# Hybrid encoder layer on one core: the last 512 tokens' MLP by rows, with seven block products for eight

## The chip, the cores and the metric

One core of one Trainium2 chip. The metric is the device time of one execution in microseconds, the median of several runs. One execution is also recorded by the hardware profiler; its span runs from the first to the last instruction.

## The reference, cut to what matters

2048 tokens of 1024 numbers pass one layer: attention and convolution side by side, cross-attention, and an MLP with 4096 hidden channels, then a final norm. All inputs and outputs are float32. The change touches the last lines only, and only for tokens 1536 to 2047:

```
u = rmsnorm(h, norm_mlp_g[l]) @ w_up[l]            # (512, 1024) @ (1024, 4096)
h = h + jnp.square(jax.nn.relu(u)) @ w_down[l]     # (512, 4096) @ (4096, 1024)
return rmsnorm(h, norm_final_g)
```

## The kernel before

The tokens are taken in four groups of 512 (`post(p)`, p = 0 to 3). In a group, `hs` holds h transposed: eight tiles, each 128 channels by 512 tokens. Attention and convolution of group p + 1 are woven between the matmuls of group p, so that the last group (p = 3) runs alone.

Every matmul of the large products is done three times (`mm3`, lines 198 to 201): each operand is split into a high part, rounded to the fast fp32r format, and a low part, the rest; high×high, high×low and low×high are summed in PSUM. `wsplit2` (line 187) splits a weight tile of 128×1024: ACT casts the high part `whi` (line 190), DVE subtracts for the low part `wlo` (line 191). `wpost` (line 1089) loads such a tile into `raw` (two buffers) by a DMA on SP's queue and splits it; `whi` and `wlo` have four buffers in all, used in turn, so that a split waits until PE has used the weight four tiles earlier. In this text that is the ring.

The MLP (line 1307 on) goes through eight groups `fg` of 512 hidden channels:

- up: four chunks of 128 channels. A chunk is 24 matmuls (eight tiles of channels, three each) of a 128×128 stationary weight against 512 moving tokens. DVE takes the maximum with zero and the row scale into `rl` (line 1321), ACT squares it (1322) and rounds it to `hhh` (1323), DVE subtracts for `hhl` (1324).
- down: eight output tiles of 12 matmuls each, weights stationary and tokens moving. DVE adds each PSUM bank to `hs` (line 1339).

So a group has 96 matmuls up and 96 down. The row scale comes from a chain at the start of the MLP: column sums on PE (`nps`, line 1174), the root on POOL and DVE (lines 173 to 180), a broadcast by PE (`nrb`, line 185), and a copy by ACT. The up matmuls don't need it; `rl` does.

In the last group of the last tokens the down product is done in two halves of 256 tokens, each followed by its final norm: squares and their sums (`add_sq`), `rstd_from`, the gain (line 1360), PE transposes back to rows (line 1367), the scaling (1369, 1371) and the stores.

The order of instructions on each engine is set by a list scheduler with its own model of time; the tile pools decide what waits for which buffer. PSUM has eight banks, which `banks` gives to kinds of tiles.

Of the kernel before, what the change touches and what calls it, by code (L numbers as in the profile page):

```python
# [10 lines left out]
F32 = mybir.dt.float32  # L11
F32R = mybir.dt.float32r
# [3 lines left out]
AF = mybir.ActivationFunctionType  # L16
ALU = mybir.AluOpType
# [4 lines left out]
P = 128  # L22
# [12 lines left out]
KC = D // P  # L35
NG = S // 512
# [7 lines left out]
def f(ap):  # L44
    return ap.bitcast(F32)


def hybrid_layer(ctx, tc, A, out):
    nc = tc.nc
    ACT, DVE, POOL, PE = nc.scalar, nc.vector, nc.gpsimd, nc.tensor  # L50
# [70 lines left out]
    ident = cst.tile([P, P], F32, name="ident")  # L121
# [41 lines left out]
    def gain(key, k):  # L163
        if key == "mem":
            return gm[:, k:k + 1]
        c = GV[key] + k
        return gv[:, c:c + 1]

    def rstd_col(dst, ss_ps, n, stat):

        v = stat.tile([P, 8], F32, tag="st_v", name="st_v", bufs=2)
        t = stat.tile([P, 8], F32, tag="st_t", name="st_t", bufs=2)
        DVE.tensor_scalar(v[:, :n], ss_ps, 1.0 / D, EPS, op0=ALU.mult, op1=ALU.add)  # L173
        newton_rsqrt(dst, v[:, :n], t[:, :n])
# [12 lines left out]
    def wsplit2(wp, raw, name, bufs=2, shape=(P, 8, P), lo_eng=None):  # L187
        hi = wp.tile(list(shape), F32R, tag="whi", name=f"whi_{name}", bufs=bufs)
        lo = wp.tile(list(shape), F32R, tag="wlo", name=f"wlo_{name}", bufs=bufs)
        ACT.copy(hi, raw)  # L190
        (lo_eng or DVE).tensor_tensor(lo, raw, f(hi), op=ALU.subtract)  # L191
        return hi, lo

    def wcols(w, c0, n=P, rows=None):
        v = w.rearrange("(k p) m -> p k m", p=P)
        return v[:, :, c0:c0 + n] if rows is None else v[:, rows[0]:rows[1], c0:c0 + n]

    def mm3(o, lh, ll, rh, rl, first, end):
        PE.matmul(o, lh, rh, start=first, stop=False)  # L199
        PE.matmul(o, lh, rl, start=False, stop=False)  # L200
        last["pe"] = PE.matmul(o, ll, rh, start=False, stop=end)  # L201
# [77 lines left out]
    wp = pool("weights")  # L279
# [829 lines left out]
    with ExitStack() as st:  # L1109
# [23 lines left out]
        first = pinned(att(0, p2_), "pe")  # L1133
# [9 lines left out]
    xp_ = pool("post_x")  # L1143
# [5 lines left out]
    def tmp(name, bufs=4, dtype=F32, shape=(P, 512)):  # L1149
        return pp.tile(list(shape), dtype, tag="tmp", name=name, bufs=bufs)  # L1150

    def xquad(q, j, name):
        return xp_.tile([P, 4, 512], F32R, tag=f"x{q}{j}", name=name)

    def ytile(q, k, name, dtype=F32R):
        return yp.tile([P, 512], dtype, tag=f"y{q}{k}", name=name)

    def add_sq(hsl, ssum, first):

        if first:  # L1160
            ACT.activation(ssum, hsl, AF.Square)
        else:
            q = tmp("sq")[:, 0:hsl.shape[1]]
            ACT.activation(q, hsl, AF.Square)
            DVE.tensor_tensor(ssum, ssum, q, op=ALU.add)
# [4 lines left out]
    def rstd_from(ssum):  # L1170
        pc = ps("c", "nps")
        n = ssum.shape[1] // P
        for j in range(n):
            PE.matmul(pc[:, j:j + 1], ssum[:, j * P:(j + 1) * P], ones[:, 0:1], start=True, stop=True)
        r = top.tile([P, 8], F32, tag="nr", name="nr", bufs=2)
        rstd_col(r[:, 0:n], pc[:, 0:n], n, top)
        return r

    def load_cat(p, half):

        d = cats.setdefault(p, {})
        for q in "hl":
            t = xquad(q, half, f"cat{q}{p}{half}")
            for e in range(4):
                d[q, 4 * (1 - half) + e] = t[:, e]
        for j in range(2):
            load_pair(p, half, j)
# [31 lines left out]
    def post(p):  # L1219
# [85 lines left out]


        FG = 8
        end = p == NG - 1
        for fg in range(FG):
            hh = {}  # L1310
            for q in "hl":
                t = xquad(q, fg % 2, f"hh{q}{p}_{fg}")
                for j in range(4):
                    hh[q, j] = t[:, j]
            for c in range(4):
                wh, wl = wpost(wcols(w_up, fg * 512 + c * P), f"u{p}{fg}_{c}")
# [4 lines left out]
                last["dve"] = DVE.scalar_tensor_tensor(r, pt, 0.0, rsb, op0=ALU.max, op1=ALU.mult)  # L1321
                ACT.activation(r, r, AF.Square)
                ACT.copy(hh["h", c], r)
                DVE.tensor_tensor(hh["l", c], r, f(hh["h", c]), op=ALU.subtract)  # L1324
                yield
            if fg == FG - 1:
                fsum = ssum_tile(f"f{p}")
                if not end:
                    load_cat(p + 1, 0)

            def down(mp2, t, w, wh, wl):
                sl = slice(t, t + w)
                for e in range(2):
                    m = 2 * mp2 + e
                    es = slice(P * e, P * e + P)
                    pt = ps("mm", "dn")[:, 0:w]
                    for k in range(4):
                        mm3(pt, wh[:, k, es], wl[:, k, es], hh["h", k][:, sl], hh["l", k][:, sl], k == 0, k == 3)
                    last["dve"] = DVE.tensor_tensor(hs[m][:, sl], hs[m][:, sl], pt, op=ALU.add)  # L1339
                    if fg == FG - 1:  # L1340
                        add_sq(hs[m][:, sl], fsum[:, sl], m == 0)

            wd = []
            for mp2 in range(4):
                wd.append(wpost(wcols(w_down, mp2 * 256, 256, (4 * fg, 4 * fg + 4)), f"d{p}{fg}_{mp2}", (P, 4, 256)))
                if fg == FG - 1 and end:
                    continue
                down(mp2, 0, 512, *wd[-1])
                yield


        fin = {}

        def final(t, w):
            r = rstd_from(fsum[:, t:t + w])
            sl = slice(t, t + w)
            for k in range(KC):
                if t == 0:
                    fin[k] = ytile("h", k, f"fin{p}_{k}", F32)
                DVE.tensor_scalar(fin[k][:, sl], hs[k][:, sl], gain("final", k), None, op0=ALU.mult)  # L1360
            for j in range(w // P):
                c0 = t + P * j
                for g in range(2):
                    ot = ytile("l", 2 * (c0 // P) + g, f"ot{p}{c0}{g}", F32)
                    pt = ps("T", "ot")
                    for i in range(4):
                        PE.transpose(pt[:, P * i:P * i + P], fin[4 * g + i][:, c0:c0 + P], ident)
                    if g:
                        ACT.activation(ot, pt, AF.Copy, scale=r[:, j:j + 1])
                    else:  # L1370
                        DVE.tensor_scalar(ot, pt, r[:, j:j + 1], None, op0=ALU.mult)
                    dma(out[0, 512 * p + c0:512 * p + c0 + P, 512 * g:512 * (g + 1)], ot)
                yield

        if end:
            for t in range(0, 512, 256):
                for mp2 in range(4):
                    down(mp2, t, 256, *wd[mp2])
                yield from final(t, 256)
        else:  # L1380
            load_cat(p + 1, 1)
            yield from final(0, 512)

    for p in range(NG):
        main = post(p)
# [72 lines left out]
```

## Time and profile before

| | |
|---|---|
| median of 3 runs | 2892.22 us (2890.32 to 2897.40) |
| the profiled execution | 2888.26 us, its span 2886.5 us |
| mean granted TensorE clock | 0.994 |
| busy: PE, DVE, ACT, POOL | 2826.6, 1857.6, 1166.3, 458.0 us |
| start of the last tokens' up product | 2520.93 us |
| start of their last down product | 2850.69 us |

A row of a group of instructions reads: line, engine, operation, out<-in, shape, count | busy us, mean ns of one | idle time before it and what ended that. A row of a window reads: stretch, its length, busy us (instructions) of PE, PE's weight loads, DVE, ACT and POOL, the granted TensorE clock, the share of the DMA engines in use, GB/s. A row of the timeline reads: start in us, duration in us, engine, line, operation, count, and in brackets the idle time before it with its releaser. PE is TensorE, DVE VectorE, ACT ScalarE, POOL GpSimd, SP SyncE (which issues the DMAs).

### The profile page before, as it was taken

How to read it: one execution, taken by the hardware profiler on the slowest of the kernel's cores; microseconds unless marked ns; L12 is line 12 of the kernel's file. 1: busy time of each engine (PE TensorE's matmuls, PEld its weight loads, DVE VectorE, ACT ScalarE, POOL GpSimd, SP SyncE). 2: the span in 40 equal slices, each digit the busy share in tenths (PEclk: the TensorE clock that was granted, in tenths of full speed). 3: DMA queues.
4: the chain of work that ended last, by engine and by line, in shares of the span. 5: the costliest groups of instructions: out<-in, count | busy, mean ns of one | idle time of the engine just before them, and what ended most of it. 6: DMA issues, size and time to landing. Idle time of an engine off the chain costs nothing.

```text
span 2886.5 us, 41313 instructions
## 1 busy us (share of the span) xinstructions
PE 2826.6 (98%) x15628; PEld 2376.2 (82%) x15628; DVE 1857.6 (64%) x3306; ACT 1166.3 (40%) x1988; POOL 458.0 (16%) x469
## 2 busy tenths in 40 slices
PE   8999999998999999999999999999999999999999
PEld 7878899887788888888888888888888888888887
DVE  5636535565789776557887765689876555544445
ACT  5633211475554333434543343444333433432233
POOL 1336421122102011200012012002011200000000
PEclk9999999999999999999999999999999999999999
DMA  8979845799734444554444446534543445333332
GB/s 264 295 173 228 202 132 131 182 256 247 205 102 131 135 133 123 168 160 145 121 130 130 138 117 192 175 96 128 142 127 109 139 132 175 93 90 101 96 95 74
DMA packets 598632, 433.74 MB, mean 150 GB/s; under 512 B 191550, under 2 KB 524786, under 8 KB 597921
## 3 DMA queue, kind: packets, MB, share of 16 engines
q1 hardware_dynamic: 558256, 408.21, 50.2%
q10 hardware_dynamic: 37952, 16.88, 2.4%
q0 software_dynamic: 2224, 6.01, 0.6%
q8 instruction: 123, 2.02, 0.3%
q14 instruction: 77, 0.62, 0.1%
HBM read 339.89 MB, written 91.11 MB: 149 GB/s over the span
## 4 chain that ended last, share of the span: by engine, by line
PE 82%; DVE 9%; DMA 5%; issue 2%; ACT 2%; POOL 1%; SPq 1%; POOLq 0%; DVEq 0%; ACTq 0%
PE dn L199 8%; PE dn L200 8%; PE dn L201 8%; PE up L199 7%; PE up L200 7%; PE up L201 7%; PE lin L199 4%; PE lin L201 4%; PE lin L200 4%; DVE cacc L216 3%; PE o L199 2%; PE o L200 2%; PE o L201 2%; PE xs L199 2%; PE xs L201 2%; PE xs L200 2%
## 5 line engine op out<-in xcount | busy, mean ns | idle before, releaser
L199 PE MATMUL dn<-hhh,whi_d 128*128 128x512 f32 (+1 forms) x1056 | 402.8, 392 | 7.2 <-DVE h L1339 6.1
L200 PE MATMUL dn<-hhl,whi_d 128*128 128x512 f32 (+1 forms) x1056 | 403.4, 385 | 1.1 <-DVE hhl L1324 1.1
L199 PE MATMUL up<-mh,whi_u 128*128 128x512 f32 x1024 | 402.9, 393 | 0.5 <-DVE rl L1321 0.5
L201 PE MATMUL dn<-hhh,wlo_d 128*128 128x512 f32 (+1 forms) x1056 | 402.6, 384 | 0.0
L200 PE MATMUL up<-ml,whi_u 128*128 128x512 f32 x1024 | 399.4, 390 | 1.0 <-DVE ml L1214 0.9
L201 PE MATMUL up<-mh,wlo_u 128*128 128x512 f32 x1024 | 399.7, 391 | 0.0
L216 DVE SCALAR_TENSOR_TENSOR cacc<-cu,cw,cacc 128x512 f32<-128x512 f32 x480 | 389.0, 811 | 5.5
L190 ACT CAST whi_d<-raw_d 128x1024 fp32r<-128x1024 f32 x128 | 134.6, 1052 | 418.1 <-PE up L200 378.6
L1339 DVE TENSOR_TENSOR h<-h,dn 128x512 f32<-128x512 f32 (+1 forms) x264 | 172.3, 667 | 162.9 <-PE dn L201 161.7
L190 ACT CAST whi_u<-raw_u 128x1024 fp32r<-128x1024 f32 x128 | 134.4, 1050 | 327.2 <-PE dn L200 304.1
L1321 DVE SCALAR_TENSOR_TENSOR rl<-up,ssumx 128x512 f32<-128x512 f32 x128 | 88.0, 690 | 256.9 <-PE up L201 252.6
L199 PEld LDWEIGHTS dn<-hhh,whi_d 128*128 128x128 f32 x1056 | 198.1, 189 | 47.5 <-DVE h L1339 10.2
L201 PEld LDWEIGHTS dn<-hhh,wlo_d 128*128 128x128 f32 x1056 | 198.8, 188 | 39.7
L200 PEld LDWEIGHTS dn<-hhl,whi_d 128*128 128x128 f32 x1056 | 199.3, 189 | 37.4 <-DVE hhl L1324 2.0
L200 PEld LDWEIGHTS up<-ml,whi_u 128*128 128x128 f32 x1024 | 192.4, 188 | 40.1 <-DVE ml L1214 2.3
L201 PEld LDWEIGHTS up<-mh,wlo_u 128*128 128x128 f32 x1024 | 192.2, 188 | 40.3
L199 PEld LDWEIGHTS up<-mh,whi_u 128*128 128x128 f32 x1024 | 192.4, 188 | 38.5 <-DVE rl L1321 0.9
L774 ACT ACTIVATE sm<-sm,o 128x256 f32<-128x256 f32 (+1 forms) x384 | 160.1, 466 | 126.3 <-DVE o L773 125.9
L773 DVE CUSTOM_DVE_ANT_0 sm<-s,mask 128x256 f32<-128x256 f32 (+1 forms) x384 | 128.5, 375 | 83.5 <-PE s L999 39.4
L191 DVE TENSOR_TENSOR wlo_u<-raw_u,whi_u 128x1024 fp32r<-128x1024 f32 x128 | 158.4, 1237 | 32.7 <-ACT whi_u L190 32.4
L191 DVE TENSOR_TENSOR wlo_d<-raw_d,whi_d 128x1024 fp32r<-128x1024 f32 x128 | 163.2, 1275 | 23.8 <-ACT whi_d L190 23.7
L177 POOL TENSOR_TENSOR nr<-st_v,mhalf 128x4 f32<-128x4 f32 (+1 forms) x13 | 13.0, 997 | 839.2 <-DVE st_v L173 839.2
(403 smaller groups left out, 6320.9 us busy)
## 6 DMA issues: line engine op xcount, KB each, us to landing
raw_u<-in_w_up_dram SPq DMA_DIRECT2D x128, 512.0 KB
raw_d<-in_w_down_dram SPq DMA_DIRECT2D x128, 512.0 KB
raw_o<-in_w_out_dram SPq DMA_DIRECT2D x32, 512.0 KB
raw_a<-ascr SPq DMA_DIRECT2D x32, 512.0 KB
raw_b<-bscr SPq DMA_DIRECT2D x32, 512.0 KB
k<-kscr SPq DMA_DIRECT2D x24, 512.0 KB
k<-kscr SPq DMA_DIRECT2D x8, 1152.0 KB
xn<-in_x_dram SPq DMA_DIRECT2D x32, 256.0 KB
```

Of the source, the lines that this page charges most:

```text
L177: POOL.tensor_tensor(dst, v, mhalf.to_broadcast([P, v.shape[1]]), op=ALU.pow)
L190: ACT.copy(hi, raw)
L191: (lo_eng or DVE).tensor_tensor(lo, raw, f(hi), op=ALU.subtract)
L199: PE.matmul(o, lh, rh, start=first, stop=False)
L200: PE.matmul(o, lh, rl, start=False, stop=False)
L201: last["pe"] = PE.matmul(o, ll, rh, start=False, stop=end)
L216: DVE.scalar_tensor_tensor(acc, u[:, t:t + 512], cw[:, c, t:t + 1], acc, op0=ALU.mult, op1=ALU.add)
L773: last["dve"] = DVE.tensor_tensor_reduce(dst, so, mask[:, 256 * m:256 * m + nk], 1.0, 3e38, ALU.add, ALU.min, mn)
L774: last["act"] = ACT.activation(dst, dst, AF.Exp, bias=mn, scale=-1.0)
L1321: last["dve"] = DVE.scalar_tensor_tensor(r, pt, 0.0, rsb, op0=ALU.max, op1=ALU.mult)
L1339: last["dve"] = DVE.tensor_tensor(hs[m][:, sl], hs[m][:, sl], pt, op=ALU.add)
```

## The change

The last tokens' MLP moves to a function of its own, `last_mlp`. There h is turned into rows at the start: 32 PE transposes, copied by ACT into `row(t)`, 128 tokens by 1024 channels each. The down product is then by rows: a slice of 128 tokens of the hidden tile is stationary, 512 columns of w_down are moving.

In groups 0 to 6 the down product of a group, (512 tokens × 512 hidden) by (512 hidden × 1024), is cut into blocks: A11, A12 (first 256 tokens, first and second half of the hidden channels), A21, A22, and the quarters B11, B12, B21, B22 of w_down. Seven products of 12 matmuls replace eight, in this order: A11·B11, A12·B21, S2·(B22−B12+B11), S1·(B12−B11), S3·(B22−B12), S4·B22, A22·(last difference), with S1 = A21+A22, S2 = S1−A11, S3 = A11−A21, S4 = A12−S2. Three pairs of PSUM banks serve as accumulators X, Y and Z, where Y and Z are the same two banks; X and Z go on accumulating after they have been added to rows. Fourteen DVE additions of 128×512 bring the banks to the rows.

The quarters of w_down are loaded whole, 512 KB each, into buffers of the attention that are free by now (`room`), and summed in place: four DVE subtractions of 128×1024 a group. DVE and ACT also make and split S1 to S4 from `rl` (`parts`; the low parts are tiles `hql` and `hz1x`). The first up chunk of the next group is written ahead of the seven products. Up has four banks of its own.

The last group does its down product by rows with all 96 matmuls, row tile after row tile, each followed by its norm: squares with their sum on ACT, the root, and one scaling by DVE with the gain as a row.

```diff
         FG = 8
-        end = p == NG - 1
+        if p == NG - 1:
+            last_mlp(hs, y, rsb)
+            return
...
+        banks.update(up=(4, 5, 6, 7), ux=(0, 1), uy=(2, 3), tr=(0, 1, 2, 3))
...
+        def to_rows(g):
+            t, c = divmod(g, 2)
+            pt = ps("tr", f"hT{g}")
+            for i in range(4):
+                PE.transpose(pt[:, P * i:P * i + P], hs[4 * c + i][:, P * t:P * t + P], ident)
+            ACT.copy(row(t)[:, 512 * c:512 * c + 512], pt)
...
+        def hidden(fg, c):
+            wh, wl = wpost(wcols(w_up, fg * 512 + c * P), f"u{p}{fg}_{c}")
+            pt = ps("up", "up")
             for k in range(KC):
+                mm3(pt, wh[:, k, :], wl[:, k, :], y["h", k], y["l", k], k == 0, k == KC - 1)
+                if fg == 0 and c < 2 and k % 2:
+                    to_rows(4 * c + k // 2)
...
+        def parts(rs_, c):
+            r, j = rs_[c], c % 2
+            lo, hi = r[:, 0:256], r[:, 256:512]
+            if c < 2:
+                split([x[:, j] for x in A1], lo)
+                DVE.tensor_tensor(lo, lo, hi, op=ALU.subtract)
+                split([x[:, j] for x in S3], lo)
+            else:
+                r0 = rs_[j]
+                split([x[:, j] for x in A2], r)
+                DVE.tensor_tensor(r0[:, 256:512], r0[:, 256:512], hi, op=ALU.add)
+                DVE.tensor_tensor(r0[:, 0:256], hi, r0[:, 0:256], op=ALU.subtract)
+                split([x[j] for x in S12], r0)
+                DVE.tensor_tensor(lo, lo, r0[:, 0:256], op=ALU.subtract)
+                split([x[:, j] for x in S4], lo)
...
+            X, Y, Z = ([ps(kind, "dn") for _ in range(2)] for kind in ("ux", "uy", "uy"))
+            sums = {"S2": (b[4], b[1, 1], b[0, 0]), "S1": (b[0, 0], b[0, 1], b[0, 0]), "S3": (b[0, 1], b[1, 1], b[0, 1]),
+                    "A22": (b[1, 0], b[1, 0], b[4])}
+            for n, (key, w, pts, more, t0, c0) in enumerate((
+                    ("A11", b[0, 0], X, False, 0, 0), ("A12", b[1, 0], Y, False, 0, 0),
+                    ("S2", b[4], X, True, 0, 1), ("S1", b[0, 0], Z, False, 2, 1),
+                    ("S3", b[0, 1], X, True, 2, 1), ("S4", b[1, 1], Z, True, 0, 1),
+                    ("A22", b[1, 0], X, True, 2, 0))):
...
+                wh, wl = wsplit2(wq if i % 4 > 1 else wp, w, f"d{p}{fg}_{n}", shape=(P, 2, 512))
+                for k in {0: ("S1", "S2"), 1: ("S3", "A22")}.get(n, ()):
+                    o, x, y_ = sums[k]
+                    DVE.tensor_tensor(o, x, y_, op=ALU.subtract)
+                for t in range(2):
+                    for j in range(2):
+                        mm3(pts[t], at[key](0, j, t), at[key](1, j, t), wh[:, j], wl[:, j], not more and j == 0, j == 1,
+                            more)
+                    a = row(t0 + t)[:, 512 * c0:512 * c0 + 512]
+                    last["dve"] = DVE.tensor_tensor(a, a, pts[t], op=ALU.add)
+
+        rs_ = []
+        for fg in range(FG - 1):
+            b = {4: room(4, "b")}
+            for c in range(4):
+                if c or not fg:
+                    rs_.append(hidden(fg, c))
+                for h in range(2) if 0 < c < 3 else ():
+                    b[c - 1, h] = quarter(fg, c - 1, h)
+                parts(rs_, c)
+            rs_ = [hidden(fg + 1, 0)]
+            seven(fg, b)
...
+        for t in range(4):
+            for c in range(2):
+                pt = ps("tr", "dn")
+                for k in range(4):
+                    wh, wl = ws[c][k // 2]
+                    mm3(pt, *(x[:, k, P * t:P * t + P] for x in hh), wh[:, k % 2], wl[:, k % 2], k == 0, k == 3)
+                a = row(t)[:, 512 * c:512 * c + 512]
+                DVE.tensor_tensor(a, a, pt, op=ALU.add)
+                ACT.activation(tmp("sq"), a, AF.Square, accum_out=ss[:, 2 * t + c:2 * t + c + 1])
...
+            for c in range(2):
+                a = row(t)[:, 512 * c:512 * c + 512]
+                DVE.scalar_tensor_tensor(a, a, r[:, 0:1], grow[c], op0=ALU.mult, op1=ALU.mult)
+                dma(out[0, 512 * p + P * t:512 * p + P * (t + 1), 512 * c:512 * c + 512], a, nc.scalar if c else None)
```

More of the change, by code (lines that the diff above doesn't have):

```diff
@@ L196, in wcols, with mm3 @@
         return v[:, :, c0:c0 + n] if rows is None else v[:, rows[0]:rows[1], c0:c0 + n]
[L198 to L201, printed above, removed]
+    def mm3(o, lh, ll, rh, rl, first, end, more=False):
+        PE.matmul(o, lh, rh, start=first, stop=False, skip_group_check=more)
+        PE.matmul(o, lh, rl, start=False, stop=False, skip_group_check=more)
+        last["pe"] = PE.matmul(o, ll, rh, start=False, stop=end, skip_group_check=more)
     w_in, w_out = A["w_in"][0], A["w_out"][0]
@@ L1327, in post, with down @@
                 fsum = ssum_tile(f"f{p}")
[L1328 to L1332, printed above, removed]
+                load_cat(p + 1, 0)
+            def down(mp2, wh, wl):
                 for e in range(2):
@@ L1335, in down @@
                     es = slice(P * e, P * e + P)
-                    pt = ps("mm", "dn")[:, 0:w]
+                    pt = ps("mm", "dn")
                     for k in range(4):
-                        mm3(pt, wh[:, k, es], wl[:, k, es], hh["h", k][:, sl], hh["l", k][:, sl], k == 0, k == 3)
-                    last["dve"] = DVE.tensor_tensor(hs[m][:, sl], hs[m][:, sl], pt, op=ALU.add)
+                        mm3(pt, wh[:, k, es], wl[:, k, es], hh["h", k], hh["l", k], k == 0, k == 3)
+                    last["dve"] = DVE.tensor_tensor(hs[m], hs[m], pt, op=ALU.add)
@@ L1340, in down @@
                     if fg == FG - 1:
-                        add_sq(hs[m][:, sl], fsum[:, sl], m == 0)
-            wd = []
+                        add_sq(hs[m], fsum, m == 0)
             for mp2 in range(4):
[L1345 to L1348, printed above, removed]
+                down(mp2, *wpost(wcols(w_down, mp2 * 256, 256, (4 * fg, 4 * fg + 4)), f"d{p}{fg}_{mp2}", (P, 4, 256)))
@@ L1349, in post @@
                 yield
+        load_cat(p + 1, 1)
+        r = rstd_from(fsum)
         fin = {}
-        def final(t, w):
-            r = rstd_from(fsum[:, t:t + w])
-            sl = slice(t, t + w)
-            for k in range(KC):
[L1358 to L1382, printed above, removed]
+        for k in range(KC):
+            fin[k] = ytile("h", k, f"fin{p}_{k}", F32)
+            DVE.tensor_scalar(fin[k], hs[k], gain("final", k), None, op0=ALU.mult)
+        for j in range(4):
+            c0 = P * j
+            for g in range(2):
+                ot = ytile("l", 2 * j + g, f"ot{p}{c0}{g}", F32)
+                pt = ps("T", "ot")
+                for i in range(4):
+                    PE.transpose(pt[:, P * i:P * i + P], fin[4 * g + i][:, c0:c0 + P], ident)
+                if g:
+                    ACT.activation(ot, pt, AF.Copy, scale=r[:, j:j + 1])
+                else:
+                    DVE.tensor_scalar(ot, pt, r[:, j:j + 1], None, op0=ALU.mult)
+                dma(out[0, 512 * p + c0:512 * p + c0 + P, 512 * g:512 * (g + 1)], ot)
+            yield
@@ new lines, in last_mlp, with row, split, halves @@
+    def last_mlp(hs, y, rsb):
+        FG, p = 8, NG - 1
+        banks.update(up=(4, 5, 6, 7), ux=(0, 1), uy=(2, 3), tr=(0, 1, 2, 3))
+        acc = [xp_.tile([P, 4, 512], F32, tag=f"x{q}0", name=f"rows{q}") for q in "hl"]
+        grow = [wk.tile([P, 512], F32, tag="sm", name=f"gain_row{c}", bufs=3) for c in range(2)]
+        for c in range(2):
+            dma(grow[c], A["norm_final_g"][512 * c:512 * c + 512].unsqueeze(0).to_broadcast([P, 512]))
+        def row(t):
+            return acc[t // 2][:, 2 * (t % 2):2 * (t % 2) + 2].rearrange("p a m -> p (a m)")
+        def to_rows(g):
+            t, c = divmod(g, 2)
+            pt = ps("tr", f"hT{g}")
+            for i in range(4):
+                PE.transpose(pt[:, P * i:P * i + P], hs[4 * c + i][:, P * t:P * t + P], ident)
+            ACT.copy(row(t)[:, 512 * c:512 * c + 512], pt)
+        def split(t, src):
+            ACT.copy(t[0], src)
+            DVE.tensor_tensor(t[1], src, f(t[0]), op=ALU.subtract)
+        def hidden(fg, c):
+            wh, wl = wpost(wcols(w_up, fg * 512 + c * P), f"u{p}{fg}_{c}")
+            pt = ps("up", "up")
+            for k in range(KC):
+                mm3(pt, wh[:, k, :], wl[:, k, :], y["h", k], y["l", k], k == 0, k == KC - 1)
+                if fg == 0 and c < 2 and k % 2:
+                    to_rows(4 * c + k // 2)
+            r = tmp("rl") if c else cv.tile([P, 512], F32, tag="vr", name="rl", bufs=2)
+            last["dve"] = DVE.scalar_tensor_tensor(r, pt, 0.0, rsb, op0=ALU.max, op1=ALU.mult)
+            ACT.activation(r, r, AF.Square)
+            return r
+        def halves(x):
+            return x.rearrange("p (j t) -> p j t", j=2)
+        q1 = [xquad(q, 1, f"hq{q}") for q in "hl"]
+        z1 = [[zp.tile([P, 512], F32R, tag=f"z{3 * i + n}", name=f"hz{i}{n}") for n in range(3)] for i in range(2)]
+        A1, S3 = ([halves(x[:, n]) for x in q1] for n in range(2))
+        A2 = [x[:, 2:4] for x in q1]
+        S12, S4 = [x[0:2] for x in z1], [halves(x[2]) for x in z1]
+        def parts(rs_, c):
[5 more added lines that the diff above has]
+                split([x[:, j] for x in S3], lo)
+            else:
+                r0 = rs_[j]
[5 more added lines that the diff above has]
+                split([x[:, j] for x in S4], lo)
+        def room(n, name):
+            if n < 2:
+                t = kq.tile([P, 1024], F32R, tag="k", name=name, bufs=2)
+            elif n == 2:
+                t = aq.tile([P, 1024], F32R, tag="ld", name=name)
+            elif n == 3:
+                t = aq.tile([P, 1024], F32R, tag="v2", name=name)
+            else:
+                return mask[:, 0:1024].rearrange("p (j m) -> p j m", j=2)
+            return f(t).rearrange("p (j m) -> p j m", j=2)
+        def quarter(fg, z, h):
+            t = room(2 * z + h, f"b{fg}{z}{h}")
+            dma(t, wcols(w_down, 512 * h, 512, (4 * fg + 2 * z, 4 * fg + 2 * z + 2)))
+            return t
+        def seven(fg, b):
+            left, right = slice(0, 256), slice(256, 512)
+            half = {"A11": A1, "S3": S3, "S4": S4, "A12": [x[:, :, left] for x in A2], "A22": [x[:, :, right] for x in A2]}
+            at = {k: (lambda x, j, t, k=k: half[k][x][:, j, P * t:P * t + P]) for k in half}
+            at["S2"] = lambda x, j, t: S12[x][j][:, P * t:P * t + P]
+            at["S1"] = lambda x, j, t: S12[x][j][:, 256 + P * t:256 + P * t + P]
+            X, Y, Z = ([ps(kind, "dn") for _ in range(2)] for kind in ("ux", "uy", "uy"))
[6 more added lines that the diff above has]
+                    ("A22", b[1, 0], X, True, 2, 0))):
+                i = turn_w[0]
+                turn_w[0] += 1
+                wh, wl = wsplit2(wq if i % 4 > 1 else wp, w, f"d{p}{fg}_{n}", shape=(P, 2, 512))
[19 more added lines that the diff above has]
+            seven(fg, b)
+        fg = FG - 1
+        hh = [xquad(q, 1, f"hh{q}") for q in "hl"]
+        for c in range(4):
+            r = hidden(fg, c) if c else rs_[0]
+            split([x[:, c] for x in hh], r)
+        ws = [[wpost(wcols(w_down, 512 * c, 512, (4 * fg + 2 * z, 4 * fg + 2 * z + 2)), f"d{p}{fg}_{c}{z}", (P, 2, 512))
+               for z in range(2)] for c in range(2)]
+        ss = top.tile([P, 8], F32, tag="fin", name="fin")
+        for t in range(4):
[7 more added lines that the diff above has]
+                ACT.activation(tmp("sq"), a, AF.Square, accum_out=ss[:, 2 * t + c:2 * t + c + 1])
+            sq = top.tile([P, 1], F32, tag="fsq", name="fsq", bufs=2)
+            DVE.tensor_tensor(sq, ss[:, 2 * t:2 * t + 1], ss[:, 2 * t + 1:2 * t + 2], op=ALU.add)
+            r = top.tile([P, 8], F32, tag="nr", name="nr", bufs=2)
+            rstd_col(r[:, 0:1], sq, 1, top)
+            for c in range(2):
+                a = row(t)[:, 512 * c:512 * c + 512]
+                DVE.scalar_tensor_tensor(a, a, r[:, 0:1], grow[c], op0=ALU.mult, op1=ALU.mult)
+                dma(out[0, 512 * p + P * t:512 * p + P * (t + 1), 512 * c:512 * c + 512], a, nc.scalar if c else None)
```

## The prediction

> **What bounds the kernel now.** I read the page's busy times first, then the windows of the last 512 tokens' MLP (up and down groups alternate there, nothing else is woven in), then single instructions.
>
> ```profile
> span 2886.5 us, 41313 instructions
> PE 2826.6 (98%) x15628; PEld 2376.2 (82%) x15628; DVE 1857.6 (64%) x3306; ACT 1166.3 (40%) x1988; POOL 458.0 (16%) x469
> core 0: us, PE busy (x) PEld busy (x) DVE busy (x) ACT busy (x) POOL busy (x), PEclk, DMA share, GB/s
> 2610.90:2654.40 43.50, 43.50 (x192) 35.78 (x192) 20.22 (x25) 12.85 (x17) 0.00 (x0) 1.00 0.33 97
> 2566.80 0.39 PE L199 MATMUL up<-mh,whi_u 128*128 128x512 f32 x1
> 2588.56 0.39 PE L199 MATMUL dn<-hhh,whi_d 128*128 128x512 f32 x1
> ```
>
> One window is one group: 192 matmuls in 43.50 us, PE never idle, DVE 20.22 us, ACT 12.85, a third of the DMA. The two matmul rows are the first of an up part and of the down part behind it: 96 matmuls in 21.76 us, 0.2267 us from start to start (the 0.39 overlaps). Here only fewer matmuls, or a PE wait, can move the time.
>
> **What the change removes.** In groups 0 to 6 the down product takes seven products of 12 matmuls for 96: 12 fewer in each, 84 × 0.2267 = 19.0 us. Stationary and moving operands change places, but both forms are 128×128 by 128×512, so I keep the price. The Trainium skill (TensorE: Matmul & The Clock Gate, section Back-to-back issue gap) gives about 131 ns per matmul in a sustained stream at this width; by that the 84 would be worth 11.0 us, but the rows above measure 227 ns and decide.
>
> **What it adds on DVE.** Durations by form, in this stage (the fourth row, from the attention's preparation, is the nearest for a quarter sum):
>
> ```profile
> L191 DVE TENSOR_TENSOR wlo_d<-raw_d,whi_d 128x1024 fp32r<-128x1024 f32 x32 | 39.2, 1225 | 11.2 <-ACT whi_d L190 11.2
> L1339 DVE TENSOR_TENSOR h<-h,dn 128x512 f32<-128x512 f32 x56 | 37.2, 686 | 74.4 <-PE dn L201 74.4
> L1324 DVE TENSOR_TENSOR hhl<-rl,hhh 128x512 fp32r<-128x512 f32 x32 | 22.1, 692 | 0.2 <-ACT hhh L1323 0.2
> L560 DVE TENSOR_TENSOR raw_v<-raw_v,vbc 128x1024 f32<-128x1024 f32 x4 | 4.9, 1218 | 15.7 <-PE vbc L185 15.7
> L1321 DVE SCALAR_TENSOR_TENSOR rl<-up,ssumx 128x512 f32<-128x512 f32 x32 | 21.9, 691 | 85.1 <-PE up L201 81.7 <-ACT ssumx L1304 3.5
> L1165 DVE TENSOR_TENSOR ssumf<-ssumf,sq 128x256 f32<-128x256 f32 x14 | 5.9, 423 | 1.5 <-ACT sq L1164 1.4
> L1322 ACT ACTIVATE rl<-rl 128x512 f32<-128x512 f32 x32 | 19.9, 625 | 0.0
> L190 ACT CAST whi_d<-raw_d 128x1024 fp32r<-128x1024 f32 x31 | 32.7, 1054 | 103.2 <-PE up L200 103.2
> ```
>
> A group of the changed kernel holds 51 DVE instructions: 4 rl (2.8 us), 11 low parts of weights (13.5), 4 sums of quarters (4.9), 14 additions into rows (9.6), 4 splits 512 wide (2.8), 14 splits and differences 256 wide (5.9). That is 39.4 us, for 20.2 before, against 180 × 0.2267 = 40.8 us of PE. Back to back they cost less than their durations:
>
> ```profile
> 2573.30 1.23 DVE L191 TENSOR_TENSOR wlo_d<-raw_d,whi_d 128x1024 fp32r<-128x1024 f32 x1 [0.17 <-ACT whi_d L190]
> 2574.48 0.69 DVE L1324 TENSOR_TENSOR hhl<-rl,hhh 128x512 fp32r<-128x512 f32 x1
> 2596.01 1.88 DVE L1339 TENSOR_TENSOR h<-h,dn 128x512 f32<-128x512 f32 x3 [4.52 <-PE dn L201]
> 2859.81 0.42 DVE L1339 TENSOR_TENSOR h<-h,dn 128x256 f32<-128x256 f32 x1
> 2860.27 0.35 DVE L1360 TENSOR_SCALAR fin<-h,gv 128x256 f32<-128x256 f32 x1
> ```
>
> 1.18 us from start to start for the 1024 wide; three 512 wide in 1.88, so 0.60; a dependent 256 wide 0.46, an independent one nearer 0.34 (both near 0.40). With these a group is 15 × 1.18 + 22 × 0.60 + 14 × 0.40 = 36.5 us. DVE fits, with a tenth to spare, if its waits don't bite. ACT has 11 casts of 1.05 and some 7 us of splits and squares, 19 us: no bound.
>
> Whether they bite I walk in the scheduler's order for groups 1 to 6, t = 0 at the first matmul of the seven products (2.72 us each). The ring of four split weights keeps each cast and low part a product or more ahead. DVE's dense stretch begins when up chunk 1 ends, at 24.5: 3 rl, 3 low parts, 4 sums, 4 wide and 10 narrow pieces, 16.5 us, so it ends near 41.2 plus half a microsecond of waits, with the next block of products due at 40.8. Nothing of its end is wanted at once: A12 is due at 43.5, S2 at 46.2. Then nine instructions (6.0 us, with waits 6.5) lead to the addition that frees the first Y bank, near 48.2; product S1 needs that bank at 40.8 + 8.2 = 49.0. A margin of 0.8 us is thin: I take 2 us lost over the six groups, with 0 and 6 as ends (0.8 of drift eats it, a further 1.0 each is lost).
>
> **Group 0** is another matter. Its rl waits for the row scale:
>
> ```profile
> 2528.86 0.94 PE L1174 MATMUL nps<-ones,ssumx 128*128 128x1 f32 x8
> 2537.29 0.60 PE L185 MATMUL nrb<-ident,nr 128*128 128x128 f32 x4
> 2538.55 1.89 DVE L1321 SCALAR_TENSOR_TENSOR rl<-up,ssumx 128x512 f32<-128x512 f32 x3 [3.46 <-ACT ssumx L1304]
> 2520.93 0.39 PE L199 MATMUL up<-mh,whi_u 128*128 128x512 f32 x1
> 2873.27 1.03 PE L1367 MATMUL ot<-ident,fin 128*128 128x128 f32 x8
> 2874.06 0.36 PE L200 MATMUL dn<-hhl,whi_d 128*128 128x256 f32 x1
> 2880.00:2883.00 3.00, 1.51 (x8) 1.11 (x8) 1.39 (x2) 1.37 (x2) 0.00 (x0) 0.72 0.46 171
> ```
>
> PE now turns hs into rows in it: 32 transposes at 0.79 / 8 = 0.1 us, 3.2 us added. In the changed order rl of chunks 1, 2 and 3 all follow up chunk 1, which PE runs last of the four: 25.5 us after the group's start (2520.93 in the trace of before): 92 matmuls 20.9, transposes 3.2, the scale's small matmuls 1.4. From there DVE must do, in order, 4 rl, 5 low parts, 4 sums, 4 row additions, 4 wide splits, the last of them hz11, the low part of S1 and S2, and 11 narrow pieces: 12 × 0.60 + 9 × 1.18 + 11 × 0.42 = 22.4 us, so it ends near 48. PE ends the next group's first up chunk at 31.8 (28 matmuls on) and products A11 and A12 at 37.2; S2 and S1 would be done at 42.7, and are done near 49. Cost 6.5, and 0.5 more for the first row addition behind it: 7 us (ends: 4, if the additions and differences overlap better; 10, if DVE's waits on ACT's casts add up). Within this gap PE stands nearly still for 5 us. The Trainium skill (TensorE: Matmul & The Clock Gate, section What's actually happening) says that the clock halves after an idle window of about 3.4 us and stays so for another; the last row, a window in which PE has waited and the granted clock is 0.72, agrees in kind. By that rule 1.7 us more would be lost, and the sum would be 2882.
>
> **The end.** The last group has no seven products: 96 full matmuls by rows for 192 of half width.
>
> ```profile
> 2850.69 0.28 PE L199 MATMUL dn<-hhh,whi_d 128*128 128x256 f32 x1
> 2876.05 0.28 PE L201 MATMUL dn<-hhh,wlo_d 128*128 128x256 f32 x1
> 2876.17 0.60 PE L1367 MATMUL ot<-ident,fin 128*128 128x128 f32 x4
> 2878.46 0.16 DVE L173 TENSOR_SCALAR st_v<-nps 128x2 f32<-128x2 f32 x1 [0.70 <-PE nps L1174]
> 2880.01 0.75 DVE L1371 TENSOR_SCALAR ot<-ot,nr 128x512 f32<-128x512 f32 x1
> 2882.36 0.75 DVE L1371 TENSOR_SCALAR ot<-ot,nr 128x512 f32<-128x512 f32 x1 [1.59 <-PE ot L1367]
> ```
>
> Before: 25.5 us from the first to the last down matmul, then 10.3 us to the span's end, 3.4 of them after the last DVE instruction. After: 96 × 0.2267 = 21.8 and 0.3 of waits; then addition 0.9 with its wait, ACT's square 0.8 with its own, sum 0.35, the root from st_v to the first scaling 1.55 as above, two scalings 1.4, and 3.4: 8.4. Gain 35.8 − 30.5 = 5.3 (ends 4 and 6.3).
>
> The six loads that move (four quarters, two gain rows) go ahead of other loads on SP, into group 2's MLP, some behind a wait for attention to leave the buffer; raw_u and raw_d queue behind them and have two chunks of 5.4 us in hand. Nothing, at most 2 us.
>
> **Sum.** 19.0 − 3.2 − 7 − 2 + 5.3 = 12.1 us. The profiled execution took 2888.26 us, 1.8 beyond its span, which gives 2876; the runs' median is 2892.2, 4 higher, so 2880.
>
> **Rivals.** *DVE becomes the bound of every group.* For it: 39.4 us of durations against 40.8, and 0.17 us before an instruction that waits (row 2573.30). If durations count whole and some 20 waits on PE and ACT cost 0.17 each, a group is 42.8 us, 2.0 over PE; six make 12 in place of my 2: gain 2, 2890. Against it: the overlap in rows 2573.30 and 2596.01. The Trainium skill (VectorE: DVE Perf Modes, section The DRAIN you can't avoid) says that the next instruction doesn't start until the pipeline is empty; those rows show starts 0.05 to 0.09 us ahead of the earlier end.
>
> *Group 0's lag comes back in each group (slower).* Mechanism: S1 and S4 write the two banks that A12 left, and wait for its additions, which stand behind DVE's splits. At 7 us in each of seven groups it costs 49: 2892 + 28 = 2920. Gain turns to loss at 3.0 us per group ((19.0 − 3.2 + 5.3) / 7) and passes 0.3% at 4.3. Against it: from group 1 on the order has hz11 ahead of the first product.
>
> *No lag anywhere* (DVE's order keeps up even in group 0): gain 21, 2871. Against it: the 22.4 us behind up chunk 1.
>
> **Chances.** Forecast 0.52, DVE bound 0.22, lag in each group 0.13, no lag 0.13. 0.3% is 8.7 us, about what a measurement of this kernel can tell from no change. The forecast passes it nine times in ten, the no-lag case always, the DVE case one time in ten: faster 0.62, same 0.25, slower 0.13. The range runs from the no-lag case's edge, 2872, to the DVE case, 2889; outside lie the slower case and the tips.
>
> **What would show it.** Right: groups 1 to 6 of 40.8 to 41.3 us with PE busy throughout; one gap of 6 to 8 us in group 0, ended by DVE's hz11 and by row additions into dn; DVE near 39 us of durations a group; the last down part under 22.5 us with about 8.4 behind it. Wrong: PE idle behind DVE's low parts or row additions in later groups, dn matmuls above 0.23 us apart with the new operands, PE waits on raw_u or raw_d near 2180 to 2310, or a halved clock beyond one window.

## The result, and the profile after

The changed kernel takes 2902.01 us (median of 9 runs, 2898.0 to 2909.29); the kernel before, run beside it, 2894.08 (9 runs, 2890.32 to 2897.4). The ratio is 1.0029, with a 95% interval of 1.0019 to 1.0040: slower by some 8 us, where 12 us of gain were forecast. The profiled execution of the changed kernel took 2909.29 us, the longest of its runs, and that of before 2888.26, shorter than all the runs beside it; so the two profiles lie 21 us apart, and differences between them are used here for places and rates, not for the ratio.

The page's first lines, windows of group 0's seven products and of two whole groups, and the last down part, all of the changed kernel:

```profile
span 2907.3 us, 41179 instructions
PE 2842.3 (98%) x15440; PEld 2361.5 (81%) x15440; DVE 1959.1 (67%) x3473; ACT 1205.6 (41%) x2055; POOL 460.9 (16%) x471
core 0: us, PE busy (x) PEld busy (x) DVE busy (x) ACT busy (x) POOL busy (x), PEclk, DMA share, GB/s
2583.91:2606.76 22.85, 19.44 (x68) 14.14 (x67) 20.64 (x32) 10.11 (x14) 0.00 (x0) 0.85 0.23 71
2633.08:2674.57 41.49, 41.49 (x182) 33.82 (x181) 36.02 (x51) 18.52 (x26) 0.00 (x0) 1.00 0.34 102
2674.57:2716.06 41.49, 41.49 (x182) 33.80 (x180) 35.89 (x51) 18.47 (x26) 0.00 (x0) 1.00 0.34 102
```
```profile
2551.39 0.40 PE L200 MATMUL up<-mh,whi_u 128*128 128x512 f32 x1
2876.64 0.39 PE L200 MATMUL dn<-whi_d,hhh 128*128 128x512 f32 x1
2898.59 0.39 PE L202 MATMUL dn<-whi_d,hhl 128*128 128x512 f32 x1
```

PE runs 188 fewer matmuls and is busy 15.7 us longer. The changed stage isn't where the time went: from its first up matmul (2551.39) to the span's end it takes 355.9 us, where before it took 365.6 (2520.93 to 2886.5). A group takes 41.49 us from the first of its products to the next group's, with PE busy throughout. Before, it took 43.69 us, counted from first up matmul to first up matmul:

```profile
2566.80:2610.49 43.69, 43.69 (x193) 35.96 (x192) 20.41 (x24) 13.03 (x17) 0.00 (x0) 1.00 0.33 97
```

But the stage begins 30.5 us later than before, although on PE, DVE and ACT the same instructions run in the same order up to there. And a group of 180 matmuls should take 40.8 us, not 41.49. Both point at the price of a single matmul. The timeline of the changed kernel shows two up chunks next to each other:

```profile
2667.14 0.39 PE L201 MATMUL up<-ml,whi_u 128*128 128x512 f32 x1
2667.37 0.39 PE L202 MATMUL up<-mh,wlo_u 128*128 128x512 f32 x1
2667.60 0.39 PE L200 MATMUL up<-mh,whi_u 128*128 128x512 f32 x1
2667.82 0.39 PE L201 MATMUL up<-ml,whi_u 128*128 128x512 f32 x1
...
2669.67 0.39 PE L200 MATMUL up<-mh,whi_u 128*128 128x512 f32 x1
2669.90 0.40 PE L201 MATMUL up<-ml,whi_u 128*128 128x512 f32 x1
2670.14 0.39 PE L202 MATMUL up<-mh,wlo_u 128*128 128x512 f32 x1
2670.37 0.39 PE L200 MATMUL up<-mh,whi_u 128*128 128x512 f32 x1
```

Read the starts, not the durations: three steps take 0.68 us in the first chunk (0.227 each) and 0.70 in the second (0.233). Same instruction, same shape, clock 1.00, no wait in between. What differs is the place of the weight tile in SBUF. The ring's four split weights lie in two pools, two tiles each: `wp` at the left end of SBUF, `wq` at the right.

The change allocates two small tiles in the pool `top`, which is the first on the right side:

```
    top.tile([P, 296], F32, name="tpad")      # in both kernels; holds nothing
...
        ss = top.tile([P, 8], F32, tag="fin", name="fin")            # new
            sq = top.tile([P, 1], F32, tag="fsq", name="fsq", bufs=2)    # new
```

They take 96 bytes of each partition (32, and two buffers of 32), and all pools stacked behind `top` move down by 96: `wq` among them, from 151584 to 151488. The left pools stay. Before, both operands of every matmul of 512 columns start at the same place modulo 128 bytes (9984 of 9984, by the allocated addresses); after, 4944 of 9996 don't. That became the theory: **such a matmul is slower when its two operands lie at different places modulo 128 bytes, and the change moved half of them apart.** Rivals: the moved loads or the new order cost the time in the program ahead of the stage; or it is the absolute place of `wq` that counts.

### The profile page after: what moved, and what is told of

The parts are those of the page before. It is cut to its first block, busy times and chain, and to the rows that moved or that the text cites. A ratio compares the mean times of both kernels' runs of the same rounds, so it can differ in the third digit from the quotient of the medians.

```text
span 2907.3 us, 41179 instructions
## 1 busy us (share of the span) xinstructions
PE 2842.3 (98%) x15440; PEld 2361.5 (81%) x15440; DVE 1959.1 (67%) x3473; ACT 1205.6 (41%) x2055; POOL 460.9 (16%) x471
## 4 chain that ended last, share of the span: by engine, by line
PE 81%; DVE 8%; DMA 5%; issue 2%; ACT 1%; SPq 1%; POOL 1%; DVEq 0%; POOLq 0%; ACTq 0%
PE dn L200 8%; PE dn L201 7%; PE dn L202 7%; PE up L200 7%; PE up L201 7%; PE up L202 7%; PE lin L200 4%; PE lin L202 3%; PE lin L201 3%; DVE cacc L217 2%; PE o L200 2%; PE o L201 2%; PE o L202 2%; PE xs L200 2%; PE xs L202 2%; PE xs L201 2%
## 5 line engine op out<-in xcount | busy, mean ns | idle before, releaser
L200 PE MATMUL dn<-hhh,whi_d 128*128 128x512 f32 x768 | 301.6, 402 | 9.0 <-DVE h L1340 8.0
L201 PE MATMUL dn<-hhl,whi_d 128*128 128x512 f32 x768 | 302.1, 396 | 0.7 <-DVE hhl L1327 0.7
L202 PE MATMUL dn<-hhh,wlo_d 128*128 128x512 f32 x768 | 300.7, 394 | 0.0
L190 ACT CAST whi_d<-raw_d 128x1024 fp32r<-128x1024 f32 x100 | 104.9, 1049 | 326.0 <-PE up L201 287.3
L1340 DVE TENSOR_TENSOR h<-h,dn 128x512 f32<-128x512 f32 x192 | 128.4, 681 | 91.1 <-PE dn L202 90.6
L1324 DVE SCALAR_TENSOR_TENSOR rl<-up,ssumx 128x512 f32<-128x512 f32 x96 | 66.0, 690 | 178.6 <-PE up L202 178.5
L200 PEld LDWEIGHTS dn<-hhh,whi_d 128*128 128x128 f32 x768 | 144.0, 188 | 41.0 <-DVE h L1340 9.8
L202 PEld LDWEIGHTS dn<-hhh,wlo_d 128*128 128x128 f32 x768 | 144.5, 188 | 32.8
L201 PEld LDWEIGHTS dn<-hhl,whi_d 128*128 128x128 f32 x768 | 144.9, 189 | 30.3 <-DVE hhl L1327 1.5
L191 DVE TENSOR_TENSOR wlo_d<-raw_d,whi_d 128x1024 fp32r<-128x1024 f32 x100 | 127.7, 1277 | 13.3 <-ACT whi_d L190 13.1
```

Of the source, the lines that this page charges most:

```text
L200: PE.matmul(o, lh, rh, start=first, stop=False, skip_group_check=more)
L201: PE.matmul(o, lh, rl, start=False, stop=False, skip_group_check=more)
L202: last["pe"] = PE.matmul(o, ll, rh, start=False, stop=end, skip_group_check=more)
L1340: last["dve"] = DVE.tensor_tensor(hs[m], hs[m], pt, op=ALU.add)
```

## The experiments

**The tiles' place put back, all else of the change kept.**

```diff
-    top.tile([P, 296], F32, name="tpad")
+    top.tile([P, 272], F32, name="tpad")
```


> The changed kernel with 24 floats less in the padding of the pool at the top of SBUF, so that all pools on that side lie again at the addresses of before (they had moved by 96 bytes); the instructions are the same. Theory (matmuls whose weights lie in the moved pool take 233.3 ns from start to start in place of 226.7, throughout the program): all 512-wide matmuls at 226.7 ns, the last tokens' up product starts at 2521 us as in before (2551 in the changed kernel), its MLP takes 351 us, median 2879 to 2880, that is 14 to 15 us under before. Rival (the six loads moved ahead on SP, or the longer program, slow what comes before the MLP): the start stays near 2551, median near 2902.

Measured: 2874.46 us (2872.75 to 2879.49), for 2890.43 of the kernel before beside it: 0.9947 (0.9935 to 0.9959). With 96 bytes of empty padding less, the changed kernel is faster than before by 16 us, where 14 to 15 were expected; the time itself is lower than the 2879 expected since before, too, ran lower beside it. The stage took the 351 us expected, but in the profile it starts at 2526 us and not at 2521 (more on that below). By the two ratios to before, 0.9947 and 1.0029, the patch is worth 0.0082 of the time, 24 us.

**The kernel before, with its right side moved by 96 bytes.**

```diff
-    top.tile([P, 296], F32, name="tpad")
+    top.tile([P, 320], F32, name="tpad")
```


> The kernel before, with 24 floats more in the same padding: its pools on that side move by 96 bytes as in the changed kernel, nothing else differs. Theory of addresses: every second pair of weight tiles at 233.3 ns, 30 us lost ahead of the last tokens' MLP and 5 in it (1536 matmuls, half of them by 6.6 ns): 2929. Rival (moved loads or longer program): 2894, no change.

Measured: 2918.5 us (2914.76 to 2922.58), 1.0095 (1.0081 to 1.0110): 28 us slower with no instruction changed. That is less than expected; 4944 matmuls at 6.6 ns would be 33 us too, and presumably some of them stand where PE waits for something else anyway, which wasn't tried. Windows of the four up chunks of one group, 24 matmuls each, two with weights in `wp` and then two in `wq`:

```profile
2602.51:2607.99 5.48, 5.48 (x25) 4.40 (x24) 2.58 (x3) 2.09 (x4) 0.00 (x0) 1.00 0.31 97
2607.99:2613.44 5.45, 5.45 (x25) 4.40 (x24) 2.57 (x3) 2.10 (x3) 0.00 (x0) 1.00 0.33 94
2613.44:2619.04 5.60, 5.60 (x27) 4.58 (x26) 2.57 (x3) 2.21 (x3) 0.00 (x0) 1.00 0.32 95
2619.04:2624.64 5.60, 5.60 (x26) 4.41 (x25) 3.02 (x4) 1.13 (x2) 0.00 (x0) 1.00 0.01 4
```

5.45 us is 227 ns a matmul, 5.60 is 233. So a loss of this size needs nothing of the new function, and the rival "loads or order" has at most a few us left to explain: in the patched change, which keeps both, the runs gain 16 us (12 to 19 by the interval), and the stage alone gains 14.4 in the profiles.

**Moved by 64 bytes** (is it the distance modulo 64 or 128?).

```diff
-    top.tile([P, 296], F32, name="tpad")
+    top.tile([P, 312], F32, name="tpad")
```


> The kernel before with 16 floats more in that padding: the pools move by 64 bytes and keep their place within 64 bytes. Theory that the place within 64 bytes counts: 2894, no change, cadence 226.7 ns. Rivals: any move of the pools costs, or the period is 128 bytes: between 2905 and 2929, cadence above 230 ns.

Measured: 2898.17 us (2894.84 to 2906.91), 1.0031 (1.0020 to 1.0042). My expectation of no change fell, so the distance doesn't count modulo 64; the rivals' bounds (above 2905 us and 230 ns) weren't reached either. 64 bytes apart costs too, but a third as much. A chunk with its weights in `wp` and one in `wq`:

```profile
2634.59:2640.03 5.44, 5.44 (x25) 4.48 (x24) 2.52 (x4) 2.15 (x4) 0.00 (x0) 1.00 0.33 95
2640.03:2645.53 5.50, 5.50 (x26) 4.54 (x25) 2.56 (x3) 1.97 (x3) 0.00 (x0) 1.00 0.33 96
```

**The left side moved by 32 bytes instead, the right side left alone** (distance, or the place of `wq`?).

```diff
-    cst.tile([P, 56], F32, name="cpad")
+    cst.tile([P, 64], F32, name="cpad")
```


> The kernel before with 8 floats more of padding in the first pool of the other side: the pools with the activations (y, hh, h) and half of the weights' ring move up by 32 bytes, those with the other half of the ring stay. If the cadence goes by how far apart the two operands of a matmul lie (within 128 bytes): matmuls whose weights moved along with y stay at 226.7 ns, those whose weights stayed lie at another distance and take 227 to 234; total 2894 to 2925. If it goes by the place of each operand for itself (the places 64 and 96 within 128 bytes being slow): both halves are slow, 228 to 240 ns, total above 2925.

**Both sides moved by the same 32 bytes.**

```diff
-    cst.tile([P, 56], F32, name="cpad")
+    cst.tile([P, 64], F32, name="cpad")
-    top.tile([P, 296], F32, name="tpad")
+    top.tile([P, 288], F32, name="tpad")
```


> The kernel before with both paddings changed, so that all pools on both sides move up by the same 32 bytes. Distances between operands stay what they were, places change from 32 to 64 within 128 bytes. By distances: no change, 2890 to 2894, cadence 226.7 ns. By places: every 512-wide matmul at 233 ns or more, 50 to 70 us lost, 2940 to 2965.

Measured: 2913.11 us (2911.18 to 2916.43), 1.0073 (1.0052 to 1.0094), with the left side alone; 2890.11 (2885.54 to 2895.0), 0.9997 (0.9986 to 1.0008), with both. The third chunk of a group, weights in `wq`, first of the left side alone and then of both:

```profile
2612.98:2618.58 5.60, 5.60 (x26) 4.66 (x25) 2.58 (x3) 2.16 (x3) 0.00 (x0) 1.00 0.32 93
```
```profile
2629.36:2634.80 5.44, 5.44 (x25) 4.50 (x24) 2.57 (x3) 2.19 (x3) 0.00 (x0) 1.00 0.34 99
```

In the first, `wq` lies where it always lay and its matmuls are slow; in the second it has moved and they are fast. The distance decides, and both times lie in the ranges expected for it. Joining each matmul of the last tokens' MLP with the allocated addresses of its operands gives the same in numbers (mean from one start to the next, gaps over 0.3 us left out):

| kernel | left / `wq`, modulo 128 | matmuls at equal places | apart |
|---|---|---|---|
| before | 32 / 32 | 1426: 227.0 ns | none |
| both moved | 64 / 64 | 1426: 227.0 ns | none |
| after | 32 / 64 | 715: 227.9 ns | 704: 233.6 ns |
| before, right 96 lower | 32 / 64 | 711: 228.3 ns | 715: 233.3 ns |
| before, left 32 higher | 64 / 32 | 711: 227.5 ns | 715: 233.2 ns |
| before, right 64 lower | 32 / 96 | 711: 227.3 ns | 715: 228.9 ns |

In the changed kernel 325 of the 704 have the moving operand 32 bytes ahead (234.0 ns) and 379 behind (233.3): which operand moves makes little difference.

Modulo 128 is a way of naming the places here, not a period that is shown. By the allocated addresses the operands at equal places lie a multiple of 512 bytes apart in all these kernels. The ones called 32 apart lie 96 bytes from such a multiple in the last tokens' MLP of the changed kernel (on either side) and of the one with its right side moved by 96, and 32 bytes from it in the one with its left side moved; they cost the same. That fits a period of 128, but two operands 128 or 256 bytes off a multiple of 512 were in no run.

**The kernel before once more**, a single execution, to see how far the start of the stage varies by itself.

> The kernel before, unchanged, for one more profile: how far the start of the last tokens' up product (2520.9 us in the first profile) moves from one execution to another without any edit. If the 5 us by which the realigned kernel's profile was late there are the moved loads, this one starts again at 2521; if they are what executions differ by (windows of halved clock at other places), it lies anywhere between 2519 and 2528.

Measured: 2895.35 us. Its first up matmul of the stage, then that of the kernel with both sides moved, the patched change and the kernel with the right side 96 bytes lower:

```profile
2527.83 0.39 PE L199 MATMUL up<-mh,whi_u 128*128 128x512 f32 x1
```
```profile
2518.06 0.39 PE L199 MATMUL up<-mh,whi_u 128*128 128x512 f32 x1
```
```profile
2526.42 0.39 PE L200 MATMUL up<-mh,whi_u 128*128 128x512 f32 x1
```
```profile
2544.84 0.40 PE L199 MATMUL up<-mh,whi_u 128*128 128x512 f32 x1
```

Kernels with equal places start the stage between 2518 and 2530, the patched change among them; those apart by 32 bytes between 2544 and 2551. Within equal places the start varies by some 12 us from profile to profile, and by 7 in the kernel before alone (2520.93 and 2527.83), as expected if executions differ by themselves. So single starts can't show a cost of a few us; the conclusions above rest on the runs and on the time from matmul to matmul. The moved loads leave no trace that exceeds this.

**The patched change with another order of its four up banks**, so that up chunk 1 of group 0 doesn't get bank 5.

```diff
-    top.tile([P, 296], F32, name="tpad")
+    top.tile([P, 272], F32, name="tpad")
...
-        banks.update(up=(4, 5, 6, 7), ux=(0, 1), uy=(2, 3), tr=(0, 1, 2, 3))
+        banks.update(up=(4, 7, 5, 6), ux=(0, 1), uy=(2, 3), tr=(0, 1, 2, 3))
```


> As the first of these runs, and the up product's PSUM banks are taken in the order 4, 7, 5, 6 for 4, 5, 6, 7, so that chunk 1 doesn't share a bank with the row scale's small matmuls and PE runs it second, not last; rl and the splits of chunks 0 and 1 can be done 9 us earlier and hz11 comes ahead of the row additions. Theory (the gap of group 0 is DVE's work piled up behind up chunk 1): the stretch from the first of the seven products to the next group's remaining up matmuls shrinks by 6 to 7 us, median 2873. Rival (the gap is DVE's total work in group 0, whatever the order): 2878 to 2880 as without the change of banks.

Measured: 2869.9 us (2862.1 to 2876.0), 0.9924 (0.9909 to 0.9940): it beats both kernels. Group 0 from its first product to the next group's, a window within it, and a later group:

```profile
2562.14:2603.06 40.92, 40.92 (x181) 33.71 (x180) 37.52 (x56) 19.78 (x28) 0.00 (x0) 1.00 0.35 103
2564.00:2580.00 16.00, 16.00 (x72) 13.07 (x71) 16.00 (x25) 7.33 (x10) 0.00 (x0) 1.00 0.49 153
2602.30:2643.10 40.80, 40.80 (x182) 33.78 (x181) 36.76 (x54) 18.77 (x26) 0.00 (x0) 1.00 0.34 103
```

Group 0 is now as short as the later groups but for 0.12 us, and PE has no gap in it, where the patched change had the one described below. So the rival, by which DVE's total work makes the gap whatever the order, is out. Chunk 1 now runs second, so DVE and ACT spread their work over the up part. From the first up matmul to the span's end it takes 342.8 us, 22.8 less than before; the no-lag rival had 21. In the runs, beside the same runs of before, it is 4.6 us under the first patched kernel, and the intervals of the two ratios overlap (0.9909 to 0.9940, 0.9935 to 0.9959); the two profiles have 8.4 in this stage. That the gap is gone is shown by the profiles, what it is worth in the runs only roughly.

## Why the prediction was wrong

**The step that failed** is the price of the matmuls that stay. The sum counted 84 fewer matmuls at 0.2267 us, took everything outside the last tokens' MLP, the six moved loads apart, as unchanged without saying so, and kept the price inside it "since both forms are 128×128 by 128×512". Half of the matmuls, 4944 of 9996, took some 233 ns from start to start instead, through the whole program. The moved operands cost 24 us in this kernel (patched against unpatched) and 28 in the kernel before. The form was no cause: with equal places the stage's matmuls start 226.8 ns apart in the patched change and 227.0 before. The diff showed two new tiles in a pool, and I read them as scratch space only; of the prediction's signs of being wrong, two came. "dn matmuls above 0.23 us apart" is the one that bears on this step, but it named the new operands, and the up matmuls have it too. The other is the clock halved beyond one window: in the changed kernel's group 0 (row 2583.91, 0.85 granted over 22.85 us) it stayed at one half for some 6.9 us, about two windows, as below in the patched change. No rival had this mechanism, which is why the range missed as well.

**The rest of the sum** is judged from the patched change, whose matmuls have the price I used. Windows of its group 0 from the first product on, of the next two groups, and then of the gap in steps of 3.4 us:

```profile
2558.59:2582.14 23.55, 19.09 (x68) 14.14 (x66) 20.68 (x32) 10.12 (x14) 0.00 (x0) 0.86 0.23 68
2582.32:2623.12 40.80, 40.80 (x181) 33.78 (x181) 37.03 (x55) 18.54 (x25) 0.00 (x0) 1.00 0.40 117
2623.12:2663.92 40.80, 40.80 (x181) 33.78 (x181) 35.99 (x52) 18.54 (x25) 0.00 (x0) 1.00 0.35 104
...
2564.00:2567.40 3.40, 0.92 (x3) 0.37 (x2) 3.40 (x6) 1.35 (x2) 0.00 (x0) 1.00 0.41 145
2567.40:2570.80 3.40, 1.50 (x6) 0.74 (x5) 3.40 (x5) 0.62 (x1) 0.00 (x0) 0.85 0.15 26
2570.80:2574.20 3.40, 3.40 (x8) 2.72 (x9) 3.40 (x8) 0.41 (x1) 0.00 (x0) 0.50 0.78 222
2574.20:2577.60 3.40, 3.40 (x11) 2.50 (x10) 0.53 (x2) 0.18 (x1) 0.00 (x0) 0.65 0.18 70
```
```profile
2565.50 0.47 PE L200 MATMUL dn<-whi_d,hz 128*128 128x512 f32 x1 [1.31 <-DVE rowsh L1476]
2567.15 0.50 PE L200 MATMUL dn<-whi_d,hz 128*128 128x512 f32 x1 [1.17 <-DVE rowsh L1476]
2570.74 0.79 PE L200 MATMUL dn<-whi_d,hz 128*128 128x512 f32 x1 [1.26 <-ACT hz L1392]
2572.18 0.63 PE L201 MATMUL dn<-wlo_d,hz 128*128 128x512 f32 x1
2572.61 0.63 PE L200 MATMUL dn<-whi_d,hz 128*128 128x512 f32 x1
...
2847.34 0.39 PE L200 MATMUL dn<-whi_d,hhh 128*128 128x512 f32 x1
2868.87 0.39 PE L202 MATMUL dn<-whi_d,hhl 128*128 128x512 f32 x1
```

- *84 matmuls fewer, 19.0 us.* Right: a group of 180 takes 40.80 us, 2.7 less than 192 matmuls at 0.2267. The prediction took the 43.50 us of its window for a whole group; that is 192 matmuls, but a group took 43.69, with 0.2 of small gaps (last point).
- *Transposes, 3.2.* Nearly: the first product starts 32.2 us after the first up matmul (2526.42 to 2558.59), where the walk had 31.8. Less 120 matmuls (27.2) and the row scale's small ones (1.2), the transposes took 3.8.
- *Group 0's lag, 7.* It measures 8.6: 23.55 us, less 66 matmuls at 0.2267. It is where the walk put it: PE is halted by additions into rows and by the high part of S1, S2, while DVE is full until its late pieces end near 2574, 48 us after the start, as walked. By the starts of the matmuls, some 5.3 us of it are waits up to row 2570.74, and 2.8 are matmuls at half clock from there on.
- *The clock.* The granted clock falls short by 0.15, 0.50 and 0.35 of three windows, 1.0 window of 3.4 us in all, which is 6.8 us at one half; matmuls then start 0.43 us apart (rows 2572.18, 2572.61). The Trainium skill (TensorE: Matmul & The Clock Gate, section What's actually happening) says that an idle window of about 3.4 us halves the clock; here no stretch was idle: PE was busy for 0.92 us of 3.40 and then for 1.50 of 3.40, within which the clock fell. I weighed that rule at 1.7 us and left it out of the sum; the lag came out 1.6 over mine. That this is the clock's doing is likely, not shown: DVE was full until 2574, so at full clock some of the 2.8 us might have been waits. With the other order of banks, where PE has no gap, the clock stayed at 1.00 through group 0.
- *Drift of 2 us in groups 1 to 6.* None: 40.80 us from each first product to the next group's, PE without a gap. The thin margin held because DVE needed 36.0 to 37.0 us (36.5 in the walk).
- *The end, 5.3.* Right, 5.5: 21.8 us for the 96 matmuls and 8.5 behind them (2868.87 + 0.23 to the span's end at 2877.6), where the walk had 8.4; the 0.3 of waits stayed away.
- *Not in the sum:* before's stage held 2.2 us of small gaps on PE: 329.76 us from its first up to its last group's first down matmul, for 1440 matmuls (326.4) and 1.2 of small ones. They went with the old order. So 19.0 − 3.8 − 8.6 + 5.5 + 2.2 = 14.3, and the stage of the patched change took 351.2 us, 14.4 less than before.

**The rivals.** DVE didn't become the bound. By form, in the changed kernel's stage:

```profile
L191 DVE TENSOR_TENSOR wlo_d<-b,whi_d 128x1024 fp32r<-128x1024 f32 x40 | 48.9, 1222 | 4.7 <-ACT whi_d L190 4.6
L1476 DVE TENSOR_TENSOR rowsh<-rowsh,dn 128x512 f32<-128x512 f32 x56 | 36.3, 680 | 2.5 <-PE dn L202 2.5
L1470 DVE TENSOR_TENSOR b<-b,b 128x1024 f32<-128x1024 f32 x13 | 15.8, 1218 | 0.0
L1393 DVE TENSOR_TENSOR hql<-rl,hqh 128x256 fp32r<-128x256 f32 x25 | 10.4, 417 | 0.0
```

The durations are those I took (1225, 686, 1218, 423 ns) and they do overlap. The lag came back in no group: in the patched change each step from group 1's first product to group 6's takes 40.80 us, and the windows show PE busy to the last hundredth. The slow side had 0.13 in all, on that rival; the loss came on a path that none of the cases had.

**From 14 us of gain to 8 of loss.** The account that the experiments carry is that of the runs: the change with its operands kept at equal places gains 16 us, and the operands' new distance costs 24. In the profiles the stage gains 9.7 us, that is 14.4 less 4.7 for its 704 slow matmuls (704 × 6.6 ns), and starts 30.5 later. That sum of 20.8 can't be set beside the 7.9 between the medians, since the two executions lie 13.1 apart by their own position among their runs (7.3 above the median after, 5.8 below it before). Taking this off leaves 7.7, but only because the two spans differ by those amounts; it is no further evidence.

## What to carry to other kernels

A new tile is a change to every pool stacked behind it. Before pricing the edit itself, compare the allocated addresses of the large matmuls' operands before and after: how far apart the two operands of a matmul lie, modulo 128 bytes. Where this has changed, pad it back (here by the very 96 bytes) and only then judge the edit. And when a stage starts late although its predecessors' instructions are the same, read the starts of equal instructions in two places: half a dozen rows show a price that no wait does, and that the busy time only hints at (more of it, with fewer matmuls).

## What the runs showed of the hardware

Matmuls of 128×128 by 128×512 in fp32r, back to back at full clock, start 226.7 ns apart when the two operands' SBUF addresses are equal modulo 128 bytes (here always a multiple of 512 apart), about 233.3 ns when they are 32 bytes apart modulo 128 in either direction, and about 229 ns when they are 64 apart. Whether the period is 128 bytes, why 64 costs less than 32, and what other widths and types do, no run here shows. The kernel's two empty tiles, `tpad` and `cpad`, set this distance.
